# Reading the operands of the dense products in four other ways, one for each feed forward of a hybrid decoder step

## The chip, the core and the metric

The kernel runs on one core of one Trainium2 chip. The metric is the device time of one execution in microseconds (us). The kernel before takes 2806.31 us, the median of two runs (2803.17 and 2809.45).

## The reference

One inference step goes through a trunk of two layers, for a prompt of 512 tokens and for eight samples of 8 tokens each, 576 tokens in all, with the same weights. Every layer is a half feed forward, a mixer and another half feed forward. The mixer of layer 0 is gated linear attention beside a spatial gate, that of layer 1 an mLSTM. Each part has a norm ahead of it, whose scale and shift come from a vector of the sequence ("ada" in the kernel). The part that matters here is the feed forward, of which there are four:

```python
def _swiglu(x, w_gate, w_up, w_down):
    return (jax.nn.silu(x @ w_gate) * (x @ w_up)) @ w_down
...
h = _modulate(_rms_norm(x, W['ffn_norm'][l, 0]), sh1, sc1)
x = x + 0.5 * g1[:, None, :] * _swiglu(h, W['ffn_w_gate'][l, 0], W['ffn_w_up'][l, 0], W['ffn_w_down'][l, 0])
```

The width of the model is 1024 (8 blocks of 128), that of the feed forward 2816 (22 blocks of 128). All inputs and outputs are float32.

## The kernel before

Features lie on the partitions and tokens along the free dimension, so an activation is a list of tiles of 128 x 576. TensorE multiplies tiles of type float32r here. To keep the precision of float32, each factor is split into a high part and a low part, and a product is the sum of three: high weights by high activations, high weights by low activations, low weights by high activations.

`tile3` (line 196) is the inner step of all dense products. For one block of 128 x 128 weights it issues six matmuls: the three products, and for each of them the two halves of the 576 tokens, 288 columns each. Each half has its own PSUM bank: the output tile `psd` has 1024 columns in two banks, the halves are columns 224 to 511 and 512 to 799. Every matmul loads its 128 x 128 weights anew. `dense_gen` (line 214) runs over the blocks of one output tile: eight for a gate or up product, eight or seven for a piece of a down product. `pair_gen` (line 234) does two output tiles at once, for the first gate and up product of a feed forward.

Weights come from one array in memory, `wall`, which the host has put in the order in which the kernel reads it (`all_units`, line 99): each unit is up to 1024 columns wide and goes by one DMA from SP's queue into a tile `wraw` (line 171). `w_split` (line 176) cuts the unit into pieces of up to 512 columns, four blocks of 128, and makes the high part `whi` on ScalarE (line 183) and the low part `wlo` on VectorE (line 184), three pieces ahead of the product that uses them. Block j of a piece is columns 128 j to 128 j + 127.

`ffn` (line 445) is the feed forward. It runs over three groups of 8, 7 and 7 feature blocks. For each block it makes a gate product and an up product, applies SiLU on ScalarE and multiplies on VectorE, and splits the result into `hh` and `hl`. Then eight down products per group add to `x` (line 419). Between the products of the first two feed forwards a few matmuls of the ada projections (line 265) are put in. A feed forward has 44 gate and up products of 8 blocks and 8 down products of 22 blocks, 528 blocks or 3168 matmuls of `tile3`. The order of everything is the order in which the code is written; there is no planner in it.

The feed forwards are named by layer and place: (0, 0), (0, 1), (1, 0), (1, 1). The profile gives line 205 to all matmuls of `tile3`, those of the mixers among them.

Of the kernel before, what the change touches and what calls it, by code (L numbers as in the profile page):

```python
# [15 lines left out]
P = 128  # L16
# [18 lines left out]
def _lhs(w):  # L35

    k, m = w.shape
    return w.reshape(k // P, P, m).transpose(1, 0, 2).reshape(P, -1)


def ffn_units(l, i):
    f0 = 0
    for n in FGROUPS:
        for f in range(f0, f0 + n):
            cut = lambda a, key, f=f: a[key][l, i][:, f * P:(f + 1) * P]
            if f == 0:
                for h in range(2):
                    yield (KD * P, lambda a, cut=cut, h=h: np.concatenate([_lhs(cut(a, key)[h * 512:h * 512 + 512]) for key in ("ffn_w_gate", "ffn_w_up")], 1))
            else:
                for key in ("ffn_w_gate", "ffn_w_up"):  # L50
                    yield (KD * P, lambda a, cut=cut, key=key: _lhs(cut(a, key)))
        for m in range(KD):
            yield (n * P, lambda a, f0=f0, n=n, m=m: _lhs(a["ffn_w_down"][l, i][f0 * P:(f0 + n) * P, m * P:(m + 1) * P]))
        f0 += n
# [35 lines left out]
def ml_units():  # L90
    yield from pair_units("ml_w_in", 0, KS)
    for f in range(2, 32):
        yield cols_unit("ml_w_in", f * P)
    for h in range(MH):
        for m in range(0, KD, 2):
            yield (KD * P, lambda a, h=h, m=m: np.concatenate([_lhs(a["ml_w_out"][0][h * 512:h * 512 + 512, c * P:c * P + P]) for c in (m, m + 1)], 1))


def all_units():
    yield from ffn_units(0, 0)  # L100
    yield from ab_units()
    yield from ffn_units(0, 1)
    yield from ffn_units(1, 0)
    yield from ml_units()
    yield from ffn_units(1, 1)
# [8 lines left out]
def cut(t, parts):  # L114

    out, c0 = {}, 0
    for name, shape in parts.items():
        n = int(np.prod(shape))
        v = t[:, c0:c0 + n]
        if len(shape) > 1:  # L120
            ax = "abcd"[:len(shape)]
            v = v.rearrange(f"p ({' '.join(ax)}) -> p {' '.join(ax)}", **dict(zip(ax, shape)))
        out[name] = v
        c0 += n
    return out


class Trunk:
    def __init__(self, ctx, tc, ins, outs):
        self.tc, self.nc, self.ins, self.outs = tc, tc.nc, ins, outs  # L130
        pool = lambda name, bufs=1, **kw: ctx.enter_context(tc.tile_pool(name=name, bufs=bufs, **kw))
        self.const = pool("const")
        self.wp = pool("wp", 2)
        self.work = pool("work", 2)
        self.psd = pool("psd", 2, space=PSUM)
        self.psc = pool("psc", 3, space=PSUM)
        self.psa = pool("psa", 1, space=PSUM)
        c = self.const
        self.x = c.tile([P, KD, T], F32, name="x")
        self.sh = c.tile([P, 7, KD, NC], F32, name="sh")  # L140
        self.am = c.tile([P, 7, KD, NC], F32, name="am")
        self.gm = c.tile([P, 6, KD, NC], F32, name="gm")
        self.adab = c.tile([P, 160], F32, name="adab")
        self.gn = c.tile([P, 7, KD], F32, name="gn")
        self.ones = c.tile([P, P], F32, name="ones")
        self.ident = c.tile([P, P], F32, name="ident")
        self.eps = c.tile([P, 1], F32, name="eps")
        self.cs = c.tile([P, KD, 32], F32, name="cs")

        self.units, self.pieces, off = [], [], 0  # L150
        for u, (n, _) in enumerate(all_units()):
            self.units.append((off, n))
            off += P * n
            self.pieces += [(u, c0, min(512, n - c0)) for c0 in range(0, n, 512)]
        self.n_load = self.n_split = self.n_piece = 0
        self.raw, self.split = {}, {}

        self.ada_load = 0
        self.ada_tiles = {}
        self.ada = self.ada_gen()  # L160
        self.ada_done = self.ada_step = 0
        self.ada_ahead = 0
        self.queue = []
        self.cut = HT


    def w_load(self, upto):
# [30 lines left out]
    def tile3(self, ps, wh, wl, xh, xl, start, stop):  # L198

        mm = self.nc.tensor.matmul  # L200
        c = self.cut
        parts = [(slice(512 - c, 512), slice(0, c)), (slice(512, 512 + T - c), slice(c, T))]
        for j, (w, xx) in enumerate(((wh, xh), (wh, xl), (wl, xh))):
            for o, t in parts:
                mm(ps[:w.shape[1], o], w, xx[:, t], start=start and j == 0, stop=stop and j == 2)  # L205

    def psum(self):

# [5 lines left out]
    def dense_gen(self, xs, order, evac):  # L214
        ps = self.psum()
        n = len(order)
        for j in range(n):
            if j % 4 == 0:
                wh, wl = self.piece()
            c = slice(j % 4 * P, j % 4 * P + P)  # L220
            k = order[j]
            self.tile3(ps, wh[:, c], wl[:, c], xs[0][k], xs[1][k], j == 0, j == n - 1)
            if j < n - 1:
                yield
        evac(self.cols(ps))
        yield
# [7 lines left out]
    def pair_gen(self, xs, order):  # L234

        ps = [self.psum() for _ in range(2)]
        for j in range(len(order)):
            if j % 4 == 0:
                ws = [self.piece(), self.piece()]
            c = slice(j % 4 * P, j % 4 * P + P)  # L240
            for (wh, wl), p in zip(ws, ps):
                self.tile3(p, wh[:, c], wl[:, c], xs[0][order[j]], xs[1][order[j]], j == 0, j == len(order) - 1)
            yield [self.cols(p) for p in ps] if j + 1 == len(order) else []
# [203 lines left out]
    def ffn(self, l, i, ss, fills, gap):  # L447
        nc = self.nc
        left = fills
        s = l * 3 + 2 * i  # L450
        if s:
            self.norm(s, ss, mid=self.split_next)
        else:
            self.first_norm(ss)
        with ExitStack() as ctx:
            room = lambda: self.ada_pool(ctx, f"ada{l}{i}", 7, 8 * gap)
            if s == 0:
                room()
            hp = ctx.enter_context(self.phase(f"hp{l}{i}"))
            if s:  # L460
                room()
            xs = self.xk()
            f0 = 0
            for gi, n in enumerate(FGROUPS):
                hh = [hp.tile([P, T], F32R, name=f"hh{j}", tag=f"hh{j}") for j in range(n)]
                hl = [hp.tile([P, T], F32R, name=f"hl{j}", tag=f"hl{j}") for j in range(n)]
                for j in range(n):
                    if gi == 0 and j == 0:
                        pg, pu = self.dense_pair(xs, KS)
                        if self.ada_step % 10 == 8:  # L470
                            self.fill(2)
                        if fills:
                            self.ada_prefetch()
                    else:
                        pg = self.dense(xs, KS)
                    sg = hp.tile([P, T], F32, name="sg", tag="sg", bufs=2)
                    nc.scalar.activation(sg, pg, AF.Silu)  # L477
                    if gi or j:
                        n_fill = min(left, 1)
                        self.fill(n_fill)  # L480
                        left -= n_fill
                        pu = self.dense(xs, KS)
                    h = hp.tile([P, T], F32, name="h", tag="h", bufs=2)
                    nc.vector.tensor_tensor(out=h, in0=sg, in1=pu, op=ALU.mult)  # L484
                    self.hilo(h, hh[j], hl[j])
                    if gi or j:
                        n_fill = min(left, 1)
                        self.fill(n_fill)
                        left -= n_fill
                last = gi == len(FGROUPS) - 1  # L490
                if last:
                    self.log_exp()
                    ss = self.ss_tiles()
                for m in range(KD):
                    ps = self.dense((hh, hl), range(n))
                    if last and m:
                        self.sumsq(m - 1, ss)
                    self.x_add(m, ps, self.gm[:, s])
                    if last and not fills:
                        self.ada_dma(min(self.ada_load + 1, self.ada_stop))  # L500
                f0 += n
            self.finish(ss)
        return ss

# [1156 lines left out]
```

## Time and profile before

| what | value |
|---|---|
| time, median of two runs | 2806.31 us |
| time of the profiled execution | 2811.97 us |
| its span, first to last instruction | 2810.2 us |
| TensorE busy (PE) | 2734.7 us, 97% |
| weight loads busy (PEld) | 2462.3 us, 88% |
| VectorE busy (DVE) | 1264.5 us, 45% |
| ScalarE busy (ACT) | 839.0 us, 30% |
| GpSimd busy (POOL) | 193.5 us, 7% |
| mean granted TensorE clock | 0.981 |

PE stands for matmuls and PEld for the weight loads that go with them and overlap them. A matmul's record is longer than its share of the time, since matmuls are pipelined: what counts is the distance from the start of one to the start of the next. A row of the timeline gives the start, the length, the engine, the line, the operation, output and inputs by the program's names, and how many instructions are merged in it. The name `psd<-xh,whi` means that the matmul writes `psd`, moves `xh` through the array and holds `whi` as weights. A row of the windows gives the stretch, its length, and for each engine its busy time and the number of instructions.

### The profile page before, as it was taken

What the parts mean: (1) busy time and instruction counts of PE and PEld (TensorE: products, weight loads), DVE (VectorE), ACT (ScalarE), POOL (GpSimd) and SP (SyncE); (2) the same over time, 40 slices, a digit from 0 to 9 for tenths busy, and PEclk for the clock granted to TensorE, in tenths of its full rate; (3) what the DMA queues carried; (4) which work ended last, traced back from release to release, by engine and by line L of the source; (5) the groups of instructions that cost most, each with busy time, mean ns of one, the idle gap of its engine ahead of it and who ended that gap; (6) DMA issues with size and microseconds to landing.
All of it is one profiled execution on the core that took longest, in us unless ns stands there. A gap on an engine that the chain in (4) does not pass through costs nothing.

```text
span 2810.2 us, 45632 instructions
## 1 busy us (share of the span) xinstructions
PE 2734.7 (97%) x19182; PEld 2462.3 (88%) x19182; DVE 1264.5 (45%) x2442; ACT 839.0 (30%) x1508; POOL 193.5 (7%) x263
## 2 busy tenths in 40 slices
PE   6999999999999999999999999999999999999997
PEld 4899998787788999998999997998567667999997
DVE  4333334446562333345333337654765676333334
ACT  4222223432242222234222234334323324222223
POOL 1000000022110000001000004300110111000000
PEclk9999999999799999999999999999999999999999
DMA  7534224221146332223222244467885665222222
GB/s 282 215 126 136 83 82 136 69 77 41 60 164 256 136 135 83 83 83 113 83 83 77 87 141 164 151 180 236 303 307 199 236 244 192 88 85 79 84 78 73
DMA packets 114740, 388.49 MB, mean 138 GB/s; under 512 B 19416, under 2 KB 37096, under 8 KB 95720
## 3 DMA queue, kind: packets, MB, share of 16 engines
q1 hardware_dynamic: 102088, 336.62, 35.6%
q0 software_dynamic: 4880, 35.06, 3.2%
q10 hardware_dynamic: 7568, 13.90, 1.3%
q8 instruction: 151, 2.47, 0.4%
q14 instruction: 53, 0.43, 0.0%
HBM read 324.95 MB, written 60.59 MB: 137 GB/s over the span
## 4 chain that ended last, share of the span: by engine, by line
PE 90%; DVE 4%; ACT 2%; issue 1%; POOL 1%; DMA 1%; DVEq 0%; SPq 0%; ACTq 0%; POOLq 0%
PE psd L205 74%; PE psc L1498 2%; PE psd L544 2%; PE psa L265 1%; PE psc L1386 1%; PE psa L1469 1%; PE psc L1403 1%; PE psc L811 1%; DVE yn L372 1%; DMA adaw<-ada 1%; POOL qe L794 1%; DVE xl L362 1%; PE psd L1477 1%; PE psc L1352 1%; PE psd L1355 1%
## 5 line engine op out<-in xcount | busy, mean ns | idle before, releaser
L205 PE MATMUL psd<-xh,whi 128*128 128x288 f32 x3648 | 794.7, 299 | 11.5 <-ACT xh L373 7.4
L205 PE MATMUL psd<-xl,whi 128*128 128x288 f32 x3648 | 786.2, 297 | 7.5 <-DVE xl L362 7.1
L205 PE MATMUL psd<-xh,wlo 128*128 128x288 f32 x3648 | 783.8, 296 | 1.5 <-DVE wlo L184 1.5
L184 DVE TENSOR_TENSOR wlo<-wraw,whi 128x512 fp32r<-128x512 f32 (+1 forms) x696 | 459.1, 697 | 454.4 <-ACT whi L183 450.9
L205 PEld LDWEIGHTS psd<-xh,whi 128*128 128x128 f32 x3648 | 589.1, 190 | 55.3 <-issue 17.8
L205 PEld LDWEIGHTS psd<-xl,whi 128*128 128x128 f32 x3648 | 589.9, 190 | 12.7 <-DVE xl L362 12.0
L205 PEld LDWEIGHTS psd<-xh,wlo 128*128 128x128 f32 x3648 | 590.2, 190 | 1.8 <-DVE wlo L184 1.8
L183 ACT CAST whi<-wraw 128x512 fp32r<-128x512 f32 (+1 forms) x696 | 400.1, 608 | 415.2 <-PE psd L205 374.8
L205 PE MATMUL psd<-hh,wlo 128*128 128x288 f32 x1408 | 301.4, 295 | 0.0
L205 PE MATMUL psd<-hh,whi 128*128 128x288 f32 x1408 | 301.3, 295 | 0.0
L205 PE MATMUL psd<-hl,whi 128*128 128x288 f32 x1408 | 300.9, 295 | 0.0
L419 DVE SCALAR_TENSOR_TENSOR x<-psd,gm,x 128x512 f32<-128x512 f32 x136 | 102.1, 751 | 356.5 <-PE psd L205 356.5
L205 PEld LDWEIGHTS psd<-hh,whi 128*128 128x128 f32 x1408 | 226.6, 188 | 1.7 <-issue 1.7
L205 PEld LDWEIGHTS psd<-hl,whi 128*128 128x128 f32 x1408 | 226.5, 188 | 0.0
L205 PEld LDWEIGHTS psd<-hh,wlo 128*128 128x128 f32 x1408 | 226.4, 188 | 0.0
L484 DVE TENSOR_TENSOR h<-sg,psd 128x576 f32<-128x576 f32 x88 | 66.4, 754 | 349.2 <-PE psd L205 349.2
L411 ACT CAST hh<-h 128x576 fp32r<-128x576 f32 x88 | 59.4, 675 | 488.8 <-DVE h L484 488.8
L477 ACT ACTIVATE sg<-psd 128x576 f32<-128x576 f32 x88 | 57.4, 652 | 360.3 <-PE psd L205 360.3
L358 POOL TENSOR_TENSOR yn<-x,rstd 128x576 f32<-128x576 f32 x30 | 49.4, 1653 | 1067.5 <-ACT rstd L386 1009.6
L412 DVE TENSOR_TENSOR hl<-h,hh 128x576 fp32r<-128x576 f32 x88 | 66.8, 759 | 65.2 <-ACT hh L411 65.2
L1481 DVE SCALAR_TENSOR_TENSOR cu<-cu,wd,psd 128x512 f32<-128x512 f32 x128 | 87.0, 742 | 18.4 <-PE psd L1477 18.4
L205 PE MATMUL psd<-hz,whi 128*128 128x288 f32 x512 | 94.6, 306 | 0.0
(331 smaller groups left out, 2257.6 us busy)
## 6 DMA issues: line engine op xcount, KB each, us to landing
wraw<-wall SPq DMA_DIRECT2D x284, 512.0 KB, 3.6
adaw<-ada SPq DMA_DIRECT2D x80, 1024.0 KB, 7.2
cu<-mC SPq DMA_DIRECT2D x32, 1024.0 KB, 5.8
Cs<-cu POOLq DMA_DIRECT2D x32, 1024.0 KB, 6.2
wraw<-wall SPq DMA_DIRECT2D x64, 448.0 KB, 3.3
szp<-zp SPq DMA_DIRECT2D x32, 256.0 KB, 2.9
bx<-sx SPq DMA_DIRECT2D x16, 512.0 KB, 6.3
zt<-szp SPq DMA_DIRECT2D x16, 512.0 KB, 7.3
```

The costliest lines, as they stand in the source:

```text
L183: nc.scalar.copy(hi[:, :n], raw)
L184: nc.vector.tensor_tensor(out=lo[:, :n], in0=raw, in1=hi[:, :n].bitcast(F32), op=ALU.subtract)
L205: mm(ps[:w.shape[1], o], w, xx[:, t], start=start and j == 0, stop=stop and j == 2)
L358: eng.tensor_tensor(out=y, in0=self.x[:, k, :], in1=rstd, op=ALU.mult)
L411: self.nc.scalar.copy(hi, y)
L412: self.nc.vector.tensor_tensor(out=lo, in0=y, in1=hi.bitcast(F32), op=ALU.subtract)
L419: nc.vector.scalar_tensor_tensor(out=xp, in0=ps[:, :TP], scalar=g[:, m, 0:1], in1=xp, op0=ALU.mult, op1=ALU.add)
L477: nc.scalar.activation(sg, pg, AF.Silu)
L484: nc.vector.tensor_tensor(out=h, in0=sg, in1=pu, op=ALU.mult)
L544: mm(ps[i], xx[:, k, self.tokens(i)], w, start=k == 0 and j == 0, stop=k == KD - 1 and j == 2)
L1481: nc.vector.scalar_tensor_tensor(out=cu[:, g], in0=cu[:, g], scalar=dec, in1=pu[:, i], op0=ALU.mult, op1=ALU.add)
L1498: mm(pc, self.v[:, s, g * P:(g + 1) * P], self.wk[:, s], start=s == 0, stop=s == 3)
```

## The change

Each of the four feed forwards reads its operands in another way; the numbers computed are the same.

- (0, 0), `backward`: the 288 activation columns of a matmul are read from the last to the first, and the 288 output columns are written from the last to the first.
- (0, 1), `woven`: the host interleaves the blocks of a piece, so that column c of block j stands at 4 c + j; the kernel reads the 128 weight columns of a block with a step of four elements. Where a piece has three blocks, the step is three.
- (1, 0), `there` and `back`: in every second block the two token halves change places, and in each block the middle product has the halves in the other order than the outer ones.
- (1, 1), `halves`: all three products of the first half, then all three of the second half, the latter in the reverse order.

The mixers' dense products keep their way of reading.

```diff
+def weave(w):
+
+    parts = [w[:, c0:c0 + 512] for c0 in range(0, w.shape[1], 512)]
+    return np.concatenate([v.reshape(P, -1, P).transpose(0, 2, 1).reshape(P, -1) for v in parts], 1)
...
-    yield from ffn_units(0, 1)
+    for n, f in ffn_units(0, 1):
+        yield n, lambda a, f=f: weave(f(a))
...
+        self.turn, self.backward, self.woven = "products", False, False
...
-        for j, (w, xx) in enumerate(((wh, xh), (wh, xl), (wl, xh))):
-            for o, t in parts:
-                mm(ps[:w.shape[1], o], w, xx[:, t], start=start and j == 0, stop=stop and j == 2)
+        products = ((wh, xh), (wh, xl), (wl, xh))
+        turns = {"products": ((0, 0), (0, 1), (1, 0), (1, 1), (2, 0), (2, 1)),
+                 "there": ((0, 0), (0, 1), (1, 1), (1, 0), (2, 0), (2, 1)),
+                 "back": ((0, 1), (0, 0), (1, 0), (1, 1), (2, 1), (2, 0)),
+                 "halves": ((0, 0), (1, 0), (2, 0), (2, 1), (1, 1), (0, 1))}[self.turn]
+        if self.turn in ("there", "back"):
+            self.turn = "back" if self.turn == "there" else "there"
+        seen = [0, 0]
+        for j, a in turns:
+            w, xx = products[j]
+            o, t = parts[a]
+            seen[a] += 1
+            out, rhs = ps[:w.shape[1], o], xx[:, t]
+            if self.backward:
+                out, rhs = out[:, ::-1], rhs[:, ::-1]
+            mm(out, w, rhs, start=start and seen[a] == 1, stop=stop and seen[a] == 3)
...
-            c = slice(j % 4 * P, j % 4 * P + P)
+            r = min(4, n - j // 4 * 4)
+            c = slice(j % 4, r * P, r) if self.woven else slice(j % 4 * P, j % 4 * P + P)
...
+            self.backward = (l, i) == (0, 0)
+            self.woven = (l, i) == (0, 1)
+            self.turn = {(1, 0): "there", (1, 1): "halves"}.get((l, i), "products")
```

A pair (j, a) in `turns` is product j for token half a. The orders of VectorE, ScalarE, GpSimd and SP's queue are the same row for row, and so are the DMAs. On TensorE only the order within a block differs. In (0, 0) and (0, 1) the same instructions stand in the same places with other steps in their operands, and in (1, 0) the rows read as before, because only the halves change places. In (1, 1) the rows differ. Here are the first blocks of its first product on TensorE before; `x2` is the two token halves:

```order
L205 MATMUL psd<-xh,whi 128x288 x2
L205 MATMUL psd<-xl,whi 128x288 x2
L205 MATMUL psd<-xh,wlo 128x288 x2
L205 MATMUL psd<-xh,whi 128x288 x2
L205 MATMUL psd<-xl,whi 128x288 x2
L205 MATMUL psd<-xh,wlo 128x288 x2
```

And here is the same place now; the line number of `tile3`'s matmul is 226 in the changed file:

```order
L226 MATMUL psd<-xh,whi 128x288
L226 MATMUL psd<-xl,whi 128x288
L226 MATMUL psd<-xh,wlo 128x288 x2
L226 MATMUL psd<-xl,whi 128x288
L226 MATMUL psd<-xh,whi 128x288 x2
L226 MATMUL psd<-xl,whi 128x288
L226 MATMUL psd<-xh,wlo 128x288 x2
```

The low activations `xl` are needed by the second matmul in place of the third, and the low weights `wlo` by the third in place of the fifth. The last matmul of a block and the first of the next both use `xh` and `whi` and are merged in one row, though the two are of different blocks and different halves.

More of the change, by code (lines that the diff above doesn't have):

```diff
@@ L239, in pair_gen @@
                 ws = [self.piece(), self.piece()]
-            c = slice(j % 4 * P, j % 4 * P + P)
+            c = slice(j % 4, 4 * P, 4) if self.woven else slice(j % 4 * P, j % 4 * P + P)
             for (wh, wl), p in zip(ws, ps):
@@ L501, in ffn @@
                 f0 += n
+            self.turn, self.backward, self.woven = "products", False, False
             self.finish(ss)
```

## The prediction

> **What bounds the kernel now.** I read the page first, its busy times and its chain of waits.
>
> ```profile
> span 2810.2 us, 45632 instructions
> PE 2734.7 (97%) x19182; PEld 2462.3 (88%) x19182; DVE 1264.5 (45%) x2442; ACT 839.0 (30%) x1508; POOL 193.5 (7%) x263
> ...
> PE 90%; DVE 4%; ACT 2%; issue 1%; POOL 1%; DMA 1%; DVEq 0%; SPq 0%; ACTq 0%; POOLq 0%
> ```
>
> TensorE is the chain for 90% of the span. So the question is what one matmul costs. The windows of the four feed forwards, for the matmuls of `tile3` alone, give the count and the time of each:
>
> ```profile
> core 0: us, PE busy (x) PEld busy (x), PEclk, DMA share, GB/s
> 37.40:481.70 444.30, 426.58 (x3168) 420.62 (x3168) 1.00 0.38 129
> 823.30:1269.00 445.70, 428.49 (x3168) 422.70 (x3168) 1.00 0.38 128
> 1279.70:1705.90 426.20, 425.10 (x3168) 424.01 (x3168) 1.00 0.31 100
> 2366.80:2793.00 426.20, 424.15 (x3168) 422.53 (x3168) 1.00 0.25 77
> ```
>
> All four have 3168 matmuls at a full granted clock (1.00) and nearly the same time; the first two windows are longer because ada matmuls lie between. Inside one, the timeline shows the beat:
>
> ```profile
> 1539.84 0.43 PE L205 MATMUL psd<-hh,wlo 128*128 128x288 f32 x2
> 1540.11 0.42 PE L205 MATMUL psd<-hh,whi 128*128 128x288 f32 x2
> 1540.37 0.43 PE L205 MATMUL psd<-hl,whi 128*128 128x288 f32 x2
> 1540.64 0.42 PE L205 MATMUL psd<-hh,wlo 128*128 128x288 f32 x2
> ```
>
> Six matmuls take 0.80 us (1539.84 to 1540.64), so one starts every 133.3 ns, whatever operand it moves. 3168 x 133.3 ns is 422 us, 99% of the 426.2 us of a window without ada work. Whatever adds a nanosecond to this beat in one feed forward adds 3.2 us to the time; the other engines have the same work in the same order.
>
> **What the beat is made of.** Two things run side by side: columns move through the array, and the next weights are loaded. For the columns, the row products of the first mixer (line 544) move 512 in place of 288, in the same type:
>
> ```profile
> 580.00 1.08 PE L544 MATMUL psd<-whi,xl 128*128 128x512 f32 x4
> 580.92 0.39 PE L544 MATMUL psc<-whi,xl 128*64 128x512 f32 x1
> 581.14 1.08 PE L544 MATMUL psd<-wlo,xh 128*128 128x512 f32 x4
> ```
>
> Five take 1.14 us, 228 ns each. So a column costs (228 - 133.3) / 224 = 0.42 ns, 288 of them 122 ns, and 11.5 ns is a fixed part. For the loads, these groups show the record of a load by its columns, and one run of matmuls that move 64 columns only and therefore go at the pace of their loads:
>
> ```profile
> L544 PEld LDWEIGHTS psd<-whi,xl 128*128 128x128 f32 x64 | 12.0, 188 | 3.5
> L544 PEld LDWEIGHTS psc<-whi,xl 128*64 128x64 f32 x16 | 2.1, 134 | 0.7
> ...
> L1262 PE MATMUL psc<-sxt,bd x64: 218/275/275, 1944.9 to 2226.3; 128*128 128x64 f32 x64
> ...
> 1944.88 1.89 PE L1262 MATMUL psc<-sxt,bd 128*128 128x64 f32 x16
> ```
>
> (188 - 134) / 64 is 0.84 ns per column, 108 ns for 128. The run agrees: 16 matmuls in 1.89 us, less the last one's 0.275, are 15 starts 108 ns apart. So a load keeps its path busy for 108 of the 133 ns, hidden behind the moving columns, with 25 ns to spare.
>
> **The change part by part.** The profiled execution took 2811.97 us (span 2810.2 and 1.8 around it), 5.7 above the median of the runs, 2806.31; sums are made against the former and then lowered by 5.7.
>
> *Weights in turns of four, (0, 1).* 8 rows x 2 groups x 3 blocks x 6 = 288 matmuls read with step three, the other 2880 with step four, 16 bytes from one element to the next. The trace has no weight load with such a step. The nearest read is VectorE's: the reduction at line 1285 reads its 256 elements with a step of 64, that at line 694 reads 512 in a row; an eight-element copy (line 1126) shows the fixed part.
>
> ```profile
> L694 DVE TENSOR_REDUCE s<-sq 128x4 f32<-128x512 f32 x4 | 2.7, 674 | 0.0
> L1285 DVE TENSOR_REDUCE nq<-t 128x64 f32<-128x256 f32 x4 | 2.4, 609 | 0.1
> L1126 DVE COPY mo<-lf 128x8 f32<-128x8 f32 x1 | 0.2, 166 | 0.0
> ```
>
> With 158 ns fixed (166 less eight elements), an element in a row costs (674 - 158) / 512 = 1.01 ns and a stepped one (609 - 158) / 256 = 1.76 ns. Part of that may be the 64 short sums in place of four; it is another engine besides. Three ways to carry it over, and a floor:
> - Loads keep 0.84 ns per column: nothing, the cover of 25 ns holds.
> - The ratio 1.75 holds: a load is 189 ns and becomes the beat, 56 ns over 133; x 2880 = 160 us.
> - The ratio is two, one extra turn for each element: 216 ns, 83 over; x 2880 = 238 us.
> - 1.76 ns holds as a time: 225 ns, 92 over; x 2880 = 265 us.
>
> A gain is excluded, since the load isn't what sets the beat now. I take two, which lies between the others, and for the 288 matmuls with step three half of what it would cost there, 288 x 83 / 2 = 12 us (0 to 24): 250 us. The cover is what decides: a load may grow by 25 ns at no cost, and only what is above that is paid.
>
> [...]
>
> *Columns backwards, (0, 0).* 3168 matmuls read and write with step minus one. No row has a negative step. The floor is nothing: each element is still next to the one before. The ceiling is that a column costs two turns in place of one, on the reading or the writing side: 122 ns more, x 3168 = 386 us. I take the floor, since neighbours stay neighbours, while the step that cost something at line 1285 goes to far elements; the ceiling stays as a rival. A gain is excluded by the 122 ns, which no other order of the columns shortens.
>
> *Halves there and back, (1, 0), and whole halves, (1, 1).* The same instructions, some of them now twice or three times in a row into the same PSUM bank. That stands in the trace: at line 787 and 788 two float32r matmuls add into one bank, and then go on to the next.
>
> ```profile
> 614.93 0.33 PE L787 MATMUL psc<-vr,lh 128*128 128x384 f32 x1
> 615.10 0.34 PE L788 MATMUL psc<-vr,ll 128*128 128x384 f32 x1
> 615.28 0.35 PE L787 MATMUL psc<-vr,lh 128*128 128x384 f32 x1
> 615.46 0.34 PE L788 MATMUL psc<-vr,ll 128*128 128x384 f32 x1
> 615.64 0.34 PE L787 MATMUL psc<-vr,lh 128*128 128x384 f32 x1
> 615.82 0.33 PE L788 MATMUL psc<-vr,ll 128*128 128x384 f32 x1
> 615.99 0.43 PE L205 MATMUL psd<-xh,whi 128*128 128x288 f32 x2
> ```
>
> From 787 to 788, same bank: 170, 180, 180 ns. From 788 on, another bank: 180, 180, 170 ns. The mean is 177 for both, so I take nothing; with times to 10 ns I allow 3 ns either way, 6336 x 3 = 19 us. The low parts are wanted one or two matmuls earlier in (1, 1), at most 267 ns. The waits that this could lengthen are small now:
>
> ```profile
> PE psd L205 <- DVE xl L362: 7.1, 16, 1.0
> ...
> PE psd L205 <- DVE wlo L184: 1.5, 1, 1.5
> ```
>
> `xl` is waited for at the start of the feed forwards, where eight tiles come one after another. Even 133 ns for each of them is 1 us, and the low weights are made pieces ahead. Nothing is moved on SP's queue or between engines.
>
> **The sum:** 2811.97 + 250 + 0 + 0 - 5.7 = 3056 us. Its own range, from the bounds of the woven loads: 160 to 265 + 24, so 2966 to 3095.
>
> **The rivals.**
> - *Not slower: the loads stay hidden.* If a stepped load takes up to 133 ns, all four ways are free: 2806, with 19 either way. For it: 25 ns of cover, and a load reads only one element in 0.84 ns where the moving side reads one in 0.42, so the reading path has been seen to go twice as fast as a load needs. It decides up to a stepped read of 1.04 ns. Against it: line 1285's 1.76 ns.
> - *Backwards columns are the cost, the loads are free:* 2811.97 + 386 - 5.7 = 3192. For it: moving columns have no cover at all; they are 122 of the 133 ns. Against it: neighbours stay neighbours. [...]
> - *Both:* 2811.97 + 250 + 386 - 5.7 = 3442.
> - *Faster:* the 11.5 ns of fixed part goes wherever matmuls no longer take turns between banks. At most 6336 x 11.5 = 73 us, so 2733. Against it: the equal 177 ns at lines 787 and 788.
>
> That the new steps come to nothing in the program would give the first rival's time, too.
>
> **How the numbers follow.** Forecast, woven loads alone: 0.31. Nothing costs anything: 0.30. Backwards alone: 0.16. Both: 0.19. Faster: 0.04. Within 2% (56 us, about what a measurement of this kernel can tell from no change) is the second case alone: 0.30. Over 2% slower are the first, third and fourth: 0.66. Faster: 0.04. To leave out no more than 2 in 10 the range has to reach from the free case, 2787, to both, 3442; only the faster case and the far side of both are out: 2787 to 3445.
>
> **What would show it.** In the window of (0, 1), PE should go from 428 us for its 3168 matmuls to about 678, with starts 216 ns apart, and load records over 290 ns (188 + 108); starts still 133 ns apart there disprove the central step. In (0, 0), (1, 0) and (1, 1) starts should stay at 133 ns. Starts of 255 ns in (0, 0) mean that backwards costs two turns. A change in (1, 0) or (1, 1) of over 3 ns per matmul would show that the order of the halves matters. The forecast is also wrong if PE waits for `xl` or `wlo` grow beyond a few us in (1, 1).

## The result and the profile after

The changed kernel takes 3110.66 us, the median of two runs (3109.29 and 3112.04), against 2806.31 before. The ratio is 1.1085, with a 95% interval of 1.1027 to 1.1142: 304 us slower. The profiled execution took 3109.29 us, 297.3 us more than that of before.

The page of the changed kernel, its busy times, says that TensorE alone is busy longer, with the same number of matmuls (19182); VectorE and ScalarE are busy as long as before:

```profile
span 3107.5 us, 45631 instructions
...
PE 3034.1 (98%) x19182; PEld 2764.3 (89%) x19182; DVE 1264.7 (41%) x2442; ACT 839.3 (27%) x1508; POOL 194.4 (6%) x263
```

The windows of the four feed forwards, for the matmuls of `tile3` alone (line 226 now), in the order (0, 0), (0, 1), (1, 0), (1, 1):

```profile
core 0: us, PE busy (x) PEld busy (x), PEclk, DMA share, GB/s
37.40:484.30 446.90, 429.31 (x3168) 423.33 (x3168) 1.00 0.37 128
826.00:1570.00 744.00, 728.45 (x3168) 724.11 (x3168) 1.00 0.23 79
1580.70:2007.00 426.30, 424.22 (x3168) 422.60 (x3168) 1.00 0.31 100
2664.00:3090.40 426.40, 424.19 (x3168) 422.60 (x3168) 1.00 0.25 77
```

The second window, that of the woven weights, has grown from 445.7 to 744.0 us, 298.3. The three others are longer by 2.6, 0.1 and 0.2 us. So one of the four ways of reading carries all but 3 us of the change, at a full granted clock (1.00). Inside that window the timeline has two beats. This is a gate or up product, where every piece has four blocks:

```profile
1380.41 0.63 PE L226 MATMUL psd<-xh,wlo 128*128 128x288 f32 x2
1380.88 0.63 PE L226 MATMUL psd<-xh,whi 128*128 128x288 f32 x2
1381.34 0.63 PE L226 MATMUL psd<-xl,whi 128*128 128x288 f32 x2
1381.81 0.63 PE L226 MATMUL psd<-xh,wlo 128*128 128x288 f32 x2
```

Six matmuls take 1.40 us, 233 ns each. And this is the end of the last down product, a piece of three blocks, read with a step of three:

```profile
1567.44 0.51 PE L226 MATMUL psd<-hh,wlo 128*128 128x288 f32 x2
1567.79 0.51 PE L226 MATMUL psd<-hh,whi 128*128 128x288 f32 x2
1568.14 0.51 PE L226 MATMUL psd<-hl,whi 128*128 128x288 f32 x2
1568.49 0.52 PE L226 MATMUL psd<-hh,wlo 128*128 128x288 f32 x2
```

Six in 1.05 us, 175 ns each. 2880 x (233.3 - 133.3) + 288 x (175 - 133.3) is 288 + 12 = 300 us, close to the window's 298. The weight loads of the down products show where the time lies. These are the records of one of their three products in that window, before, and then after (minimum, median, maximum in ns):

```profile
L205 PEld LDWEIGHTS psd<-hh,wlo x352: 187/188/192, 944.2 to 1268.6; 128*128 128x128 f32 x176
```

```profile
L226 PEld LDWEIGHTS psd<-hh,wlo x352: 261/330/330, 1022.1 to 1569.6; 128*128 128x128 f32 x176
```

A load whose record was 188 ns long now has one of 330 ns with a step of four and of 261 with a step of three.

### The profile page after: what moved, and what is told of

It reads as the page before. It is cut to its first block, busy times and chain, and to the rows that moved or that the text cites. A ratio compares the mean times of both kernels' runs of the same rounds, so it can differ in the third digit from the quotient of the medians.

```text
span 3107.5 us, 45631 instructions
## 1 busy us (share of the span) xinstructions
PE 3034.1 (98%) x19182; PEld 2764.3 (89%) x19182; DVE 1264.7 (41%) x2442; ACT 839.3 (27%) x1508; POOL 194.4 (6%) x263
## 4 chain that ended last, share of the span: by engine, by line
PE 91%; DVE 4%; ACT 1%; issue 1%; POOL 1%; DMA 1%; DVEq 0%; SPq 0%; ACTq 0%; POOLq 0%
PE psd L226 77%; PE psd L570 1%; PE psc L1524 1%; PE psa L287 1%; PE psc L1412 1%; PE psa L1495 1%; PE psc L1429 1%; PE psc L837 1%; DVE yn L394 1%; POOL qe L820 1%; DMA adaw<-ada 1%; PE psc L1378 1%; PE psd L1503 1%; PE psd L1381 0%; DVE xl L384 0%
## 5 line engine op out<-in xcount | busy, mean ns | idle before, releaser
L226 PE MATMUL psd<-xl,whi 128*128 128x288 f32 x3648 | 915.9, 317 | 7.7 <-DVE xl L384 7.3
L226 PE MATMUL psd<-xh,whi 128*128 128x288 f32 x3648 | 869.0, 319 | 10.8 <-ACT xh L395 6.7
L226 PE MATMUL psd<-xh,wlo 128*128 128x288 f32 x3648 | 856.3, 316 | 1.5 <-DVE wlo L192 1.5
L226 PEld LDWEIGHTS psd<-xh,whi 128*128 128x128 f32 x3648 | 672.3, 216 | 54.6 <-issue 17.9
L226 PEld LDWEIGHTS psd<-xl,whi 128*128 128x128 f32 x3648 | 692.4, 216 | 13.0 <-DVE xl L384 12.4
L226 PEld LDWEIGHTS psd<-xh,wlo 128*128 128x128 f32 x3648 | 673.0, 216 | 1.8 <-DVE wlo L192 1.8
L226 PE MATMUL psd<-hl,whi 128*128 128x288 f32 x1408 | 360.1, 317 | 0.0
L226 PEld LDWEIGHTS psd<-hl,whi 128*128 128x128 f32 x1408 | 272.2, 219 | 0.0
L226 PEld LDWEIGHTS psd<-hh,whi 128*128 128x128 f32 x1408 | 262.9, 219 | 1.7 <-issue 1.7
L226 PEld LDWEIGHTS psd<-hh,wlo 128*128 128x128 f32 x1408 | 262.7, 219 | 0.0
```

Of the source, the lines that this page charges most:

```text
L226: mm(out, w, rhs, start=start and seen[a] == 1, stop=stop and seen[a] == 3)
```

## The experiments

Each kernel below was timed once, except the first, which has 10 runs. The kernel before lay between 2803 and 2812 us in all of its runs, so a difference below some 10 us is nothing that a single run can tell.

### The other three ways without the woven weights

```diff
     for n, f in ffn_units(0, 1):
-        yield n, lambda a, f=f: weave(f(a))
+        yield n, f
...
-            self.woven = (l, i) == (0, 1)
+            self.woven = False
```

> Columns backwards, halves there and back and whole halves in turn stay; only the woven weights of feed forward (0, 1) are undone. If the woven loads are the whole cost: the time of before within 0.7% (2806 +- 19 us), every feed forward at 133 to 134 ns per matmul. If the three other ways cost or save something that the windows hide: outside of that.

It took 2808.95 us (median of 10 runs) beside 2809.11 for the kernel before on the same chip, a ratio over all runs of 1.0008, interval 0.9996 to 1.0020. Its windows, in the same order, now for all instructions and not those of `tile3` alone:

```profile
core 0: us, PE busy (x) PEld busy (x) DVE busy (x) ACT busy (x) POOL busy (x), PEclk, DMA share, GB/s
37.40:484.30 446.90, 444.62 (x3305) 426.95 (x3306) 159.32 (x291) 119.41 (x203) 4.26 (x3) 0.99 0.37 128
825.20:1270.90 445.70, 444.87 (x3310) 428.11 (x3311) 159.76 (x296) 118.77 (x202) 4.27 (x3) 1.00 0.37 129
1281.40:1707.70 426.30, 424.49 (x3173) 423.27 (x3174) 156.97 (x282) 118.79 (x202) 5.05 (x5) 1.00 0.31 100
2362.70:2789.20 426.50, 424.57 (x3174) 423.38 (x3175) 155.89 (x280) 117.70 (x200) 4.29 (x3) 1.00 0.25 77
```

The second window is back at its 445.7 us, and the total doesn't differ from before by anything that 10 runs can tell. Halves there and back and halves in turn cost nothing that shows: their windows, 426.3 and 426.5 us, are within 0.3 us of before (426.2 both). Columns backwards are nearly so. From the start of the first matmul of (0, 0) to the start of the last, the two kernels that read backwards take 446.6 us (37.3 to 483.9 in both), and the kernel before and the eight runs below 443.7 to 443.9. That is 2.8 us, 0.9 ns a matmul, which the totals are too coarse to show; its cause was not followed. The rest of the change is the woven weights.

### Weights with a step of two

The two beats of the change give one price if four neighbouring float32, 16 bytes, are counted as one unit, the "line" of the expectations from here on. The 128 columns of a load touch 128 such groups with a step of four and 96 with a step of three, and 233.3 / 128 and 175 / 96 are both 1.82 ns. Four is the smallest group for which this holds: of groups of two or three, both steps touch 128. The unit is an estimate from these two beats; for the loads no run shows it directly, and a price by the distance between the columns would fit them as well.

```diff
-    parts = [w[:, c0:c0 + 512] for c0 in range(0, w.shape[1], 512)]
+    parts = [w[:, c0:c0 + 256] for c0 in range(0, w.shape[1], 256)]
...
-            r = min(4, n - j // 4 * 4)
-            c = slice(j % 4, r * P, r) if self.woven else ...
+            r, q = min(2, n - j // 2 * 2), j % 4 // 2 * 256
+            c = slice(q + j % 2, q + r * P, r) if self.woven else ...
```

> The woven weights alone, with two blocks interleaved in place of four, so 128 columns are read with a step of two elements; all else as before. Theory A, a load pays for each change of a 16-byte line: 4-step 128 lines in 233 ns, 3-step 96 lines in 175 ns, both 1.82 ns a line, so 2-step 64 lines are 117 ns, under the beat of 133: about 2806 us, load records near 190 to 200 ns. Theory B, a price for every stepped element whatever the step: a load of well over 133 ns, at 175 ns as with step three some +130 us, at 233 ns +315 us.

It took 2806.57 us beside 2809.11. (The third block of a piece of three is alone there and is read without a step.) The load records of one product of the down products of (0, 1):

```profile
L226 PEld LDWEIGHTS psd<-hh,wlo x352: 187/196/198, 941.1 to 1263.7; 128*128 128x128 f32 x176
```

The load records are 8 ns longer, 196 in place of 188, and the time doesn't show it: the run agrees with theory A, and theory B falls. How long such a load keeps its path busy can only be estimated, since it doesn't set the beat. A record is longer than that time by 80 ns for neighbours (188 less the 108 of the prediction), by 86 with a step of three (261 less 175) and by 97 with a step of four (330 less 233). Step two lies between the first two of these, so it is 110 to 116 ns for 128 columns by this estimate, where theory A said 117. This is also the direct sight of the cover: growth of a load within the beat of 133 ns cost nothing here.

### The woven layout, put in order again by the split

If the load is the place of the cost, then the interleaved layout in memory is harmless as long as another engine takes the step.

```diff
+            ho, l_o = hi[:, :n], lo[:, :n]
+            if u in self.apart:
+                raw = raw.rearrange("p (c j) -> p j c", j=n // P)
+                ho, l_o = (v.rearrange("p (j c) -> p j c", j=n // P) for v in (ho, l_o))
-            nc.scalar.copy(hi[:, :n], raw)
-            nc.vector.tensor_tensor(out=lo[:, :n], in0=raw, in1=hi[:, :n].bitcast(F32), op=ALU.subtract)
+            nc.scalar.copy(ho, raw)
+            nc.vector.tensor_tensor(out=l_o, in0=raw, in1=ho.bitcast(F32), op=ALU.subtract)
```

`self.apart` is the range of the units of (0, 1); its loads read neighbours.

> The weights of (0, 1) lie interleaved by four in memory as in the change, but ScalarE and VectorE read them with the step when they split them into high and low parts and write the blocks in a row again, so that TensorE's loads read neighbours. The other three feed forwards as before. If the cost is the stepped read of TensorE's loads alone: 2806 us, the split's instructions on the two engines longer (VectorE's 697 ns towards 1070 at 1.76 ns an element), hidden by 3.2 us of matmuls for each piece. If the layout in memory or the transfers cost: a good part of the +300 us stays.

It took 2812.37 us beside 2810.57. The split's instructions between 850 and 1200 us, on VectorE and ScalarE, first before and then in this run:

```profile
L184 DVE TENSOR_TENSOR wlo<-wraw,whi x104: 550/684/694, 856.0 to 1194.0; 128x512 fp32r<-128x512 f32 x96, 128x384 fp32r<-128x384 f32 x8
...
L183 ACT CAST whi<-wraw x104: 511/619/623, 855.2 to 1193.3; 128x512 fp32r<-128x512 f32 x96, 128x384 fp32r<-128x384 f32 x8
```

```profile
L198 DVE TENSOR_TENSOR wlo<-wraw,whi x106: 668/1087/1109, 848.9 to 1195.9; 128x512 fp32r<-128x512 f32 x98, 128x384 fp32r<-128x384 f32 x8
...
L197 ACT CAST whi<-wraw x104: 707/1117/1160, 856.2 to 1194.8; 128x512 fp32r<-128x512 f32 x96, 128x384 fp32r<-128x384 f32 x8
```

The median subtraction goes from 684 to 1087 ns (the 697 of the expectation is the mean over the whole kernel) and the median cast from 619 to 1117. Both engines now pay for the step, and both have the time: they were busy for 45% and 30% of the span before, and the total is 1.8 us from that of before. The 300 us are gone with the same layout in memory, so neither layout nor transfers had a part in them.

### Moving columns with a step of two

The remaining question was why the columns, which have no cover, did not mind being read backwards, and whether they mind a step at all.

```diff
+        if self.other:
+            parts = [(o, slice(a, T, 2)) for a, (o, _) in enumerate(parts)]
...
-                    nc.vector.tensor_tensor(out=h, in0=sg, in1=pu, op=ALU.mult)
+                    nc.vector.tensor_tensor(out=back(h), in0=two(sg), in1=two(pu), op=ALU.mult)
```

`self.other` holds during the gate and up products of (0, 1); `two` and `back` are views that put the tokens in order.

> Weights as before. In the gate and up products of (0, 1), 2112 matmuls, the two halves are the even and the odd tokens, so the 288 moving columns are read with a step of two, 144 lines in place of 72; the product at the SiLU puts the tokens back in order. Theory A1, the moving side pays 1.8 ns a line as the loads do, so that the plain beat (72 lines, 133 ns) is already this price: 262 ns a matmul, +270 us. Theory A2, the beat is the array plus a fixed part and two columns to a line are enough: 133 ns, +0 us.

It took 3064.72 us beside 2809.11. Its beat there:

```profile
1001.46 0.69 PE L208 MATMUL psd<-xl,whi 128*128 128x288 f32 x2
1001.97 0.69 PE L208 MATMUL psd<-xh,wlo 128*128 128x288 f32 x2
1002.48 0.69 PE L208 MATMUL psd<-xh,whi 128*128 128x288 f32 x2
1002.99 0.69 PE L208 MATMUL psd<-xl,whi 128*128 128x288 f32 x2
```

Six in 1.53 us, 255 ns. The step that cost nothing on the weights nearly doubles the beat on the moving side, from 133 to 255 ns, and 2112 x 122 = 258 us are the 256 that the run lost. Theory A2 falls, and at this point theory A1 looked right.

### Moving one column over and over

```diff
+                rhs = xx[:, t]
+                if self.other:
+                    rhs = rhs[:, :1].to_broadcast([P, HT])
-                mm(ps[:w.shape[1], o], w, xx[:, t], start=start and j == 0, stop=stop and j == 2)
+                mm(ps[:w.shape[1], o], w, rhs, start=start and j == 0, stop=stop and j == 2)
```

> In (0, 1) every matmul moves the first column of its half 288 times (step zero), so that almost nothing has to be read; the products of the other columns are left out. Theory A1, the plain beat is the price of 72 lines: the beat falls to the array's own, 120 to 125 ns, -25 to -40 us. Theory A2, a fixed part beside the array: the beat stays at 133 ns and the time at 2806 us.

The kernel leaves out the products of all other columns; only its time is of use. It took 2778.46 us beside 2809.11, and the beat in (0, 1) is:

```profile
1000.99 0.41 PE L209 MATMUL psd<-xl,whi 128*128 128x288 f32 x2
1001.24 0.41 PE L209 MATMUL psd<-xh,wlo 128*128 128x288 f32 x2
1001.48 0.41 PE L209 MATMUL psd<-xh,whi 128*128 128x288 f32 x2
1001.73 0.41 PE L209 MATMUL psd<-xl,whi 128*128 128x288 f32 x2
```

Six in 0.74 us, 123 ns. So 10 of the 11.5 ns that the prediction called a fixed part go away when there is hardly anything to read, as A1 had expected (120 to 125 ns). These 10 ns of the plain beat hang on the moving read.

### Moving columns with a step of four

```diff
-            parts = [(o, slice(a, T, 2)) for a, (o, _) in enumerate(parts)]
+            xh, xl = (v.rearrange("p (a n f) -> p a f n", a=2, f=4) for v in (xh, xl))
+            parts = [(o, a) for a, (o, _) in enumerate(parts)]
```

> As the run with the step of two on the moving side, but each gate and up matmul of (0, 1) reads its own half's 288 columns in four turns with a step of four: 288 line changes in place of 72 (plain) and 144 (step two). Theory A1, a price per line (133.3 ns at 72, 256.2 at 144, so 1.71 ns a line and 10 ns fixed): 502 ns a matmul, 2112 x 369 = +779 us, about 3588 us. Theory A3, any step over one halves the rate and no more: 256 ns as with step two, about 3065 us.

It took 3077.78 us beside 2810.74; six matmuls take 1.57 us, 262 ns each:

```profile
1001.31 0.71 PE L209 MATMUL psd<-xh,wlo 128*128 128x288 f32 x2
1001.84 0.71 PE L209 MATMUL psd<-xh,whi 128*128 128x288 f32 x2
1002.36 0.71 PE L209 MATMUL psd<-xl,whi 128*128 128x288 f32 x2
1002.88 0.71 PE L209 MATMUL psd<-xh,wlo 128*128 128x288 f32 x2
```

Theory A1 falls: by its count there are twice as many line changes as with step two, and they cost 7 ns more, 262 against 255, where A1 said 502. The 1.82 ns per line that fit the loads do not carry over to the moving side.

### Pairs, and groups of four

Two runs then asked how many neighbours must stay together. The halves are read in two turns, first the even groups of the half, then the odd ones; a group is two columns in one run (`f=2`) and four in the other (`f=4`).

```diff
+            pick = lambda v, a: v[:, a * HT:(a + 1) * HT].rearrange("p (n g f) -> p g n f", g=2, f=2)
+            xh, xl = ([pick(v, a) for a in range(2)] for v in (xh, xl))
```

> As the runs with steps of two and four on the moving side, but neighbours stay together in pairs: in the gate and up products of (0, 1) each matmul reads columns 0, 1, 4, 5, 8, 9 and so on, and then 2, 3, 6, 7. Theory C, the moving side fetches eight bytes at a time for 0.9 ns (144 fetches plain: 133 ns; 288 with step two or four: 256 and 262 ns): 144 fetches, 133 to 140 ns a matmul, 2806 to 2822 us. Theory A3, anything but one run of neighbours goes at half rate: 256 to 262 ns, about 3065 to 3078 us. Theory A1, a price per 16-byte line, already contradicted by step four: 144 line changes, 256 ns.

> As the run with pairs, but four neighbours, one 16-byte line, stay together: columns 0 to 3, 8 to 11 and so on, then 4 to 7, 12 to 15. 72 lines are read, each once and whole, in another order. Theory A3, only one long run of neighbours goes at full rate: 256 to 262 ns a matmul, about 3061 to 3078 us. Theory A4, whole lines go at full rate wherever they lie: 133 to 140 ns, about 2806 to 2822 us.

The pairs took 3060.69 us beside 2803.32: six in 1.54 us, 257 ns.

```profile
1001.03 0.69 PE L210 MATMUL psd<-xh,wlo 128*128 128x288 f32 x2
1001.54 0.69 PE L210 MATMUL psd<-xh,whi 128*128 128x288 f32 x2
1002.05 0.69 PE L210 MATMUL psd<-xl,whi 128*128 128x288 f32 x2
1002.57 0.69 PE L210 MATMUL psd<-xh,wlo 128*128 128x288 f32 x2
```

The groups of four took 2803.25 us beside 2810.57: six in 0.79 us, 132 ns.

```profile
1000.94 0.42 PE L210 MATMUL psd<-xl,whi 128*128 128x288 f32 x2
1001.20 0.42 PE L210 MATMUL psd<-xh,wlo 128*128 128x288 f32 x2
1001.46 0.43 PE L210 MATMUL psd<-xh,whi 128*128 128x288 f32 x2
1001.73 0.42 PE L210 MATMUL psd<-xl,whi 128*128 128x288 f32 x2
```

Theory C (eight bytes at a time) falls with the pairs, and theory A3 (one long run only) with the groups of four. The two runs go through the columns in the same two turns and differ in the size of the group alone, so the read in two turns cost nothing in itself (132 ns). What is left is A4, for groups of four: whole groups went at full rate, 132 ns or 0.46 a column, also out of order, and a read that takes one or two of a group's four columns goes at 0.89 to 0.91 ns a column, about half that rate. Three of four was not tried on the moving side, nor were four neighbours whose first column is no multiple of four, so whether their place or only the run of four counts is open.

### Both sides stepped

The step of two on the moving side, and the weights woven by four as in the change.

```diff
+    for n, f in ffn_units(0, 1):
+        yield n, lambda a, f=f: weave(f(a))
...
+            parts = [(o, slice(a, T, 2)) for a, (o, _) in enumerate(parts)]
```

> In (0, 1) the weights woven by four as in the change, and the moving columns of the gate and up products read with a step of two. Theory of the cover, the slower of the two reads sets the beat: 256 ns in gate and up (a load of 233 is hidden), 218 ns in the down products as in the change: 3065 + 1056 x 84 ns = about 3153 us. Rival, the two reads share one path and their lines add up (144 + 128): gate and up at 256 + 100 = 356 ns or more, about 3365 us.

It took 3163.95 us beside 2810.74. Gate and up products:

```profile
1001.42 0.71 PE L215 MATMUL psd<-xh,wlo 128*128 128x288 f32 x2
1001.94 0.71 PE L215 MATMUL psd<-xh,whi 128*128 128x288 f32 x2
1002.46 0.71 PE L215 MATMUL psd<-xl,whi 128*128 128x288 f32 x2
1002.98 0.71 PE L215 MATMUL psd<-xh,wlo 128*128 128x288 f32 x2
```

Six in 1.56 us, 260 ns, where the moving step alone has 255. The same woven loads that cost 100 ns a matmul in the change cost 5 here, because the columns take longer than they do. So the slower of the two reads, 255 and 233 ns, all but set the beat here; they didn't add up, which would have given 356. What the 5 ns that are left are made of was not followed.

## Why the prediction was right, and where it was off

The step that decided was right: the woven loads grow past the beat of 133 ns and become the beat, in (0, 1) alone, and the other ways cost next to nothing. The time, 3110.66 us, is 55 us over the forecast of 3056 and 16 over the upper end of the forecast's own range (2966 to 3095). It lies in the stated range, 2787 to 3445, but that range holds the free case and both costs together as well, and the chance given to the woven loads alone, 0.31, was hardly above the 0.30 of the free case, so the total says little. The signs named beforehand say more: in the window of (0, 1), starts 233 ns apart (216 expected), PE at 728 us (678) and load records of 330 ns (over 290), while the starts elsewhere stayed within 1 ns or so of 133.

- **What bounds the kernel.** The window of (0, 1) grew by 298 us and the span by 297. What the beat gained went straight into the time.
- **The cover.** Confirmed from both sides: the load records of step two grew by 8 ns inside the cover for nothing, and the woven loads of 233 ns were hidden again under columns of 255 (a beat of 260). The point of decision, 1.04 ns a column, lies between step two (about 0.9 by the estimate) and step three (1.37, 175 ns for 128 columns). The smaller steps are not free in themselves: step three lifts the loads over the beat, to 175 ns, and step two takes the moving columns from 133 to 255.
- **The size of the term, which was off.** The prediction gave three ways to carry VectorE's row over and took the ratio of two, 83 ns a matmul and 238 us, because it lay between the others. Measured were 100 ns and 288 us. The absolute time would have come nearer: 1.76 ns an element at line 1285, 1.82 on TensorE (233.3 / 128). Even the prediction's bound for it, 265 us, was 23 short. The run that put the layout in order again bears the row out: with the 158 ns of fixed part, VectorE's subtraction takes (1087 - 158) / 512 = 1.81 ns an element with a step of four, without the short sums of line 1285. The doubt about that row was unfounded. That the two engines agree was not known beforehand, and it is no general price of a step: the moving columns of TensorE pay 0.91 ns with the same step of four.
- **The 288 matmuls with step three.** Half of the price of step four was taken, 41.5 ns; 41.7 were measured. That is luck. Half was a middle between bounds, and the measured share is 41.7 of 100; a share taken too large met a price taken too small.
- **Columns backwards.** The floor was taken because neighbours stay neighbours, and it nearly holds: 2.8 us where the forecast had nothing and the rival 386. The records of the matmuls in (0, 0) changed a little, from a median of 293 to 298 ns for `psd<-xh,whi`, in both kernels that read backwards, so the step did reach the program. The groups of four fit in on the reading side: whole groups out of order went at full rate (132 ns). The rival with 386 us had the right price for the wrong pattern: 122 ns a matmul is what a step of two costs the moving side. On the writing side, whether PSUM minds any pattern but this one is open.
- **The first rival,** that the loads stay hidden, rested on the reading path having been seen at twice the speed that a load needs. That speed, 0.42 ns a column, was measured on the moving read of neighbours. The loads have a price of their own: with a step of four they took 1.82 ns a column, the moving side 0.91, so the one read told nothing of the other.
- **Halves in another order.** Free (windows 0.1 and 0.2 us longer), as the equal 177 ns at lines 787 and 788 said, and the new kernel has no more waits for `xl` than before (7.3 us in 16 waits, 7.1 before).
- **The faster rival** took the 11.5 ns as the price of changing banks. That is refuted: the halves in turn change banks less often and keep the beat (426.4 us for the window beside 426.2), and moving one column over and over removes 10 ns, from 133 to 123, with all the bank changes left. The prediction had also called the 11.5 ns fixed; most of it goes away with the reading of the moving columns.

## What to carry to other kernels

Before giving a TensorE operand a step, ask which of its two reads has cover: a weight load of 128 columns that lies behind 133 ns of columns took a step of two float32 for nothing here (2806.57 us beside 2809.11), while the moving side, without cover, went from 132 ns with whole groups of four neighbours to 255 to 262 when they were split. When a price must be carried from one engine to another, try the time per element as well as the ratio to the plain read, and put both in the range. An interleaved layout in memory need not reach TensorE: if another engine touches the data anyway and has time, let that engine take the step, as the split did here (2812.37 us beside 2810.57).

## What the runs showed of the hardware that was not expected

- The weight loads of these runs, 128 columns of float32r, fit the slower of 0.84 ns a column and 1.82 ns for each group of four float32 touched, an estimate from the beats: 108 ns for 128 neighbours, 110 to 116 (an estimate) with step two, 175 with step three (96 groups), 233 with step four (128 groups). Up to a step of four a price by the distance from the first column to the last fits as well, since groups and distance grow together there; a step of eight could tell them apart and was not run. VectorE's rows, 1.76 ns an element with a step of 64 (line 1285) and 1.81 with one of four, give no sign that distance counts there; for the loads it is open.
- The moving side behaved otherwise: 132 to 133 ns for 288 neighbours, read forwards, backwards or in whole groups of four out of order, and 255 to 262 ns with one or two columns taken from a group at a time. Step four cost 7 ns more than step two there, though it goes from group to group twice as often.
- With one column moved 288 times the beat is 123 ns. So 10 of the 133 ns of a plain float32r matmul of 288 columns hang on the moving read, in a kernel in which PE is busy for 97% of the span. No way to use this was found.
